# State-space output computed by channels, with rearranged first loads and last stretch, in a one-core hybrid encoder block

## The chip, the core and the metric

The kernel runs on one core of a Trainium2 chip. The metric is device time in microseconds of one execution, the median over runs. TensorE (PE in the rows) has its own weight loads (PEld); VectorE is DVE, ScalarE is ACT, GpSimd is POOL, and SyncE (SP) issues most transfers (SPq is its queue).

## The reference, cut to what matters

One encoder block over 512 tokens of width 1024, batch 1, all float32. Two token mixers work side by side on the normalised input: grouped attention (8 query heads, 2 key/value heads, 64 wide) and a two-directional state-space mixer (16 heads of 64, 2 groups, state 128, chunks of 128 tokens). Gates merge them, and a SwiGLU feed-forward part follows.

```python
y_diag = jnp.einsum("bcgls,bcgrls,bcsgrp->bclgrp", cb, decay_in, xd)
...
y_off = jnp.einsum("bclgn,bcgrpn,bcgrl->bclgrp", cc, prev, jnp.exp(a_cs))
return (y_diag + y_off).reshape(b, l, g, r, p)
...
y = y_fwd + y_bwd + d_skip.astype(f32).reshape(shp)[..., None] * xs
return rms_norm(y * jax.nn.silu(z), ssd_norm)
...
mixed = (g_attn * attn_out + g_ssd * ssd_out) @ w_out[i]
x = x + rms_norm(mixed, norm1_post[i])
gate, up = jnp.split(rms_norm(x, norm2_pre[i]) @ w_gate_up[i], 2, axis=-1)
x = x + rms_norm((jax.nn.silu(gate) * up) @ w_down[i], norm2_post[i])
```

## The kernel before

Dense products of float32 are made as three fp32r products (low by high, high by low, high by high: `mm3`, L178 to L180), so each operand is split in a high part (a cast, L144 for weights) and a low part (a subtraction, L149, on DVE or POOL; or a negation on ACT, L146, and an accumulating DMA that POOL issues, L147). Weights come in on SP's queue (L101). A unit of such work is 128 rows by 512 columns.

The stages stand in this order: query projection with norm statistics (`xT` loads, L249 to L283), keys and values, the convolution branch, the z projection woven into attention, the state-space stage (`ssd`) with gate projections as filler, `ssd_transposed` and `attn_proj`, `mix`, `out_proj`, the feed-forward part (fewer products by sums of blocks, L972), and `w_down` (seven products of blocks, L1125), which ends with the norm and the residual. A scheduler sets the order up to `mix`; from `out_proj` on PE's order is written by hand and the other engines' is the scheduler's. Within one engine instructions run in that order, so a wait stops whatever stands behind it.

**z projection** (`zproj`): tokens on partitions, tiles `z[t][n]`. **Attention**: after two heads' probabilities are transposed (L653), eight products of probabilities and values (L677) write one bank, two heads in the two halves of its 128 partitions.

**State-space stage**: there are 16 units (4 chunks, 2 groups, 2 halves of four heads). A unit makes a decay matrix E: a sum R on DVE (L757, every other unit), two products on 32 rows (L763), a selection (L766), an exponential on ACT (L767) and the product with `cb` (L768). Then four products (L815) have E as weights and 64 columns of `xs` moving, into token-major bank `sc`. Every second unit `ssd_combine` adds the states' part: per direction a product (L779), a multiplication t1 (L781, DVE), an addition to y (L782, POOL), then y plus the bank (L783) and z times y (L785). 

**`ssd_transposed`**: 32 transposes (L832) turn the result to channel-major, the split follows (L835, L836), and `attn_proj` runs between.

**The last stretch of `w_down`**: the sixth product's weights come by `raw` when they are needed. For each half token block the results are added in (`add`, L1245), squared (L155), scaled by the gain (L1257 and L1264, mostly on POOL), and `finish` makes the root (L190 to L209) and the residual (L1270) and stores.

Of the kernel before, what the change touches and what calls it, by code (L numbers as in the profile page):

```python
# [8 lines left out]
F32 = mybir.dt.float32  # L9
# [10 lines left out]
P = 128  # L20
# [40 lines left out]
class Block:  # L61
# [41 lines left out]
    def weights(self):  # L103
# [6 lines left out]
        for n in range(2):  # L110
            for i in range(4):
                yield a["w_z"][n, i], 1024, "gv"[n]
# [44 lines left out]
    def row_rstd(self, ss, dst, sqrt=False):  # L157

        V = self.V
        s2 = ss.rearrange("p (t i) -> p t i", i=2)  # L160
        v = self.tiny(NT, "rv")
        V.tensor_tensor(v, s2[:, :, 0], s2[:, :, 1], ALU.add)
        V.tensor_scalar(v, v, 1.0 / D, EPS, ALU.mult, ALU.add)
# [13 lines left out]
    def mm3(self, o, lh, ll, rh, rl, first, last):  # L177
        self.T.matmul(o, ll, rh, start=first, stop=False)  # L178
        self.T.matmul(o, lh, rl, start=False, stop=False)  # L179
        self.last_mm = self.T.matmul(o, lh, rh, start=False, stop=last)  # L180
# [53 lines left out]
    def setup(self):  # L234
# [12 lines left out]
        for k in range(KD):  # L247
            xT.append(self.slot("t", [S], name="xT"))
            self.load(xT[k], a["xT"][k * P : k * P + P])  # L249
# [13 lines left out]
        with self.tc.manual_schedule(engines=engines):  # L263
# [6 lines left out]
            for k in range(KD):  # L270
                xh.append(self.slot("q", [S], F32R, "xh"))
                xl.append(self.slot("x", [S], F32R, "xl"))
                A.mul(xh[k], xT[k], gcol[:, k : k + 1])
                A.copy(half(wh, k), half(raws, k))
                V.scalar_tensor_tensor(xl[k], xT[k], gcol[:, k : k + 1], xh[k].bitcast(F32), ALU.mult, ALU.subtract)
                last = (V if k < 1 else G).tensor_tensor(half(wl, k), half(raws, k), half(wh, k).bitcast(F32), ALU.subtract)
# [5 lines left out]
            for k in range(KD):  # L282
                for t in range(NT):  # L283
                    tok = slice(t * P, t * P + P)
                    self.mm3(pq[t], xh[k][:, tok], xl[k][:, tok], half(wh, k), half(wl, k), k == 0, k == KD - 1)
# [322 lines left out]
    def zproj(self):  # L608
        self.z = [[None, None] for _ in range(NT)]
        for n in range(2):  # L610
            w = [self.wnext(3 - i) for i in range(4)]
            for t in range(NT):
                p = self.ps("mm")
                for k in range(KD):
                    hh, hl = self.hk(self.hT, k, slice(t * P, t * P + P))
                    wh, wl = w[k // 2]
                    c = slice((k % 2) * 512, (k % 2) * 512 + 512)
                    self.mm3(p, hh, hl, wh[:, c], wl[:, c], k == 0, k == KD - 1)
                    if k == 3:
                        yield 2.6  # L620
# [835 lines left out]
```

## Time and profile before

| what | value |
| --- | --- |
| median of 3 runs | 820.66 us (820.65 to 821.98) |
| the profiled execution | 821.49 us, span 819.7 us |
| PE busy | 801.7 us, 98% of the span |
| DVE, ACT, POOL busy | 584.1, 458.9, 209.6 us |
| granted TensorE clock | 0.995 over the span, 1.00 in each stretch up to 810 us |
| chain that ended last | PE 84%, DVE 6%, ACT 3%, DMA 3%, issue 2%, POOL 2% |
| state-space stage with gates | 232 to 345 us |
| transposes and `attn_proj` | 345 to 378 us |
| last PE instruction ends | 808.8 us |

PE is busy nearly throughout, so the time is PE's work plus the start, the waits and the tail. A PE row's length is longer than the distance to the next start, since matmuls overlap; the distances between starts are what an instruction costs. An x2 in a row of PE counts records: one float32 product makes two.

### The profile page before, as it was taken

The page shows a single profiled execution, that of the slowest core. Times are in us where ns is not written, and L with a number is a line of the kernel's source. Part 1 is how long each engine was busy: PE and PEld are TensorE (multiplying, and loading weights), DVE is VectorE, ACT ScalarE, POOL GpSimd, SP SyncE. Part 2 cuts the span into 40 slices and gives each one's busy share as a digit, 9 for nine tenths or more (in the row PEclk, how much of TensorE's full clock was granted, in tenths as well). Part 3 has the DMA queues.
Part 4 walks back from the last instruction along what each step waited for, and adds up shares of the span by engine and source line. Part 5 has one row for each costly group of instructions (what it writes and reads, how often), then busy time and mean ns, then how long its engine had stood idle before and what let it go on. Part 6 is the DMA issues. An engine that isn't in the chain of part 4 may idle for free.

```text
span 819.7 us, 12211 instructions
## 1 busy us (share of the span) xinstructions
PE 801.7 (98%) x4522; PEld 674.1 (82%) x4522; DVE 584.1 (71%) x1000; ACT 458.9 (56%) x834; POOL 209.6 (26%) x161
## 2 busy tenths in 40 slices
PE   8999999999999999999999999999999999999994
PEld 7788888676667777677888899999999999888883
DVE  2979776856524556691973888888888887928987
ACT  7677875645744433285333655555555555546762
POOL 2444340000032354458450021000000000132611
PEclk9999999999999999999999999999999999999997
DMA  8657820300675653257254453666667675899542
GB/s 306 209 155 173 186 79 26 103 1 30 168 191 149 157 142 78 76 154 246 95 175 161 153 163 101 183 181 181 180 180 185 177 183 162 314 271 238 95 87 102
DMA packets 48651, 126.93 MB, mean 155 GB/s; under 512 B 5457, under 2 KB 5841, under 8 KB 48593
## 3 DMA queue, kind: packets, MB, share of 16 engines
q1 hardware_dynamic: 38048, 95.46, 33.8%
q0 software_dynamic: 10544, 30.71, 21.7%
q8 instruction: 35, 0.57, 0.3%
q14 instruction: 24, 0.19, 0.1%
HBM read 117.76 MB, written 8.39 MB: 154 GB/s over the span
## 4 chain that ended last, share of the span: by engine, by line
PE 84%; DVE 6%; ACT 3%; DMA 3%; issue 2%; POOL 2%; SPq 0%; DVEq 0%; ACTq 0%; POOLq 0%
PE sa L972 10%; PE mm L178 8%; PE mm L179 8%; PE mm L180 8%; PE sc L972 7%; PE sa L1125 4%; PE sb L1125 4%; PE mm L972 3%; PE sb L972 3%; PE mm L1125 3%; PE sc L178 3%; PE sc L179 3%; PE sc L180 3%; PE sc L677 2%; PE sb L653 2%
## 5 line engine op out<-in xcount | busy, mean ns | idle before, releaser
L144 ACT CAST whi<-raw 128x1024 fp32r<-128x1024 f32 (+3 forms) x69 | 68.1, 992 | 20.3 <-PE sc L180 9.5
L149 POOL TENSOR_TENSOR wlo<-raw,whi 128x1024 fp32r<-128x1024 f32 (+1 forms) x28 | 58.2, 2082 | 65.4 <-ACT whi L144 63.6
L178 PE MATMUL mm<-hT,wlo 128*128 128x512 f32 x176 | 73.3, 416 | 0.0
L1023 POOL DMA_DIRECT2D raw<-in_w_gu x19 | 16.3, 859 | 211.8 <-DMA raw<-in_w_gu 89.6
L180 PE MATMUL mm<-hT,whi 128*128 128x512 f32 x176 | 69.4, 394 | 0.0
L179 PE MATMUL mm<-hT,whi 128*128 128x512 f32 x176 | 68.8, 391 | 0.0
L1029 DVE TENSOR_TENSOR wlo<-raw,whi 128x512 fp32r<-128x512 f32 (+1 forms) x57 | 49.1, 889 | 17.0 <-ACT whi L1028 16.7
L1028 ACT CAST whi<-raw 128x512 fp32r<-128x512 f32 (+1 forms) x57 | 41.7, 762 | 34.5 <-PE mm L972 14.7
L972 PE MATMUL sa<-R,whi 128*128 128x256 f32 x304 | 56.4, 283 | 0.0
L147 POOL DMA_DIRECT2D wlo<-in_w_g x14 | 12.1, 862 | 145.1 <-PE mm L179 81.1
L972 PEld LDWEIGHTS sa<-R,whi 128*128 128x128 f32 x304 | 47.4, 192 | 0.0
L972 PE MATMUL sa<-R,wlo 128*128 128x256 f32 x152 | 43.0, 283 | 0.0
L178 PEld LDWEIGHTS mm<-hT,wlo 128*128 128x128 f32 x176 | 33.1, 188 | 9.4 <-issue 3.2
L179 PEld LDWEIGHTS mm<-hT,whi 128*128 128x128 f32 x176 | 33.1, 188 | 8.7 <-issue 2.4
L180 PEld LDWEIGHTS mm<-hT,whi 128*128 128x128 f32 x176 | 33.0, 188 | 7.5 <-issue 0.5
L146 ACT ACTIVATE wlo<-raw 128x1024 fp32r<-128x1024 f32 (+1 forms) x24 | 25.1, 1047 | 24.4 <-PE mm L178 24.3
L149 DVE TENSOR_TENSOR wlo<-raw,whi 128x1024 fp32r<-128x1024 f32 (+1 forms) x17 | 20.2, 1201 | 16.6 <-ACT whi L144 10.1
L972 PE MATMUL sa<-h2T,b 128*128 128x256 f32 x228 | 30.5, 283 | 0.0
L1196 DVE TENSOR_TENSOR wlo<-ch,whi 128x1024 fp32r<-128x1024 f32 x16 | 20.4, 1281 | 13.2 <-ACT whi L1195 13.1
L972 PEld LDWEIGHTS sa<-R,wlo 128*128 128x128 f32 x152 | 29.2, 192 | 0.0
L638 DVE TENSOR_REDUCE nmax<-sa 128x1 f32<-128x512 f32 x32 | 21.6, 687 | 10.2 <-PE sa L636 9.8
L155 ACT ACTIVATE junk<-z 128x512 bf16<-128x512 f32 x8 | 5.0, 628 | 42.6 <-DVE z L785 42.5
(475 smaller groups left out, 2571.4 us busy)
## 6 DMA issues: line engine op xcount, KB each, us to landing
raw<-in_w_gu SPq DMA_DIRECT2D x44, 512.0 KB, 4.4
raw<-in_w_gu POOLq DMA_DIRECT2D x19, 512.0 KB, 5.3
raw<-in_w_g SPq DMA_DIRECT2D x16, 512.0 KB, 5.9
wlo<-in_w_g POOLq DMA_DIRECT2D x14, 512.0 KB, 6.7
raw<-in_w_dn SPq DMA_DIRECT2D x14, 512.0 KB, 7.6
raw<-in_w_xbc SPq DMA_DIRECT2D x12, 512.0 KB, 5.2
ch<-in_w_dn POOLq DMA_DIRECT2D x12, 512.0 KB, 7.8
b<-in_w_gu SPq DMA_DIRECT2D x19, 256.0 KB, 5.4
```

Source lines behind the costliest of these rows:

```text
L144: self.A.copy(h[:, :n], raw[:, :n])
L146: self.A.mul(l[:, :n], raw[:, :n], -1.0)
L149: e.tensor_tensor(l[:, :n], raw[:, :n], h[:, :n].bitcast(F32), ALU.subtract)
L178: self.T.matmul(o, ll, rh, start=first, stop=False)
L179: self.T.matmul(o, lh, rl, start=False, stop=False)
L180: self.last_mm = self.T.matmul(o, lh, rh, start=False, stop=last)
L638: V.tensor_reduce(nmax, ps, AX.X, ALU.max, negate=True)
L972: self.T.matmul(dst, x, y[:, k], start=start and k == 0 and i == 0, stop=k == 3 and i == 2, skip_group_check=True)
L1028: A.copy(dst[0], src)
L1029: lo.tensor_tensor(dst[1], src, dst[0].bitcast(F32), ALU.subtract)
L1125: self.T.matmul(o, x, y, start=start and i == 0, stop=i == 2, skip_group_check=True)
L1196: V.tensor_tensor(l, src, h.bitcast(F32), ALU.subtract)
```

## The change

1. **First loads**: the first half of `w_q` is loaded ahead of the first `xT`, `norm1_pre` goes through POOL's queue, the first block is split weights first, and its first matmul is high by high.
2. **z projection** by channels: eight tiles `z[j]` of 128 channels by 512 tokens.
3. **Attention**: the eight products of one bank are issued only after the last transposition.
4. **State-space stage**: E moves (128 columns) past stationary `xs` (64 channels), two heads in the two column halves of PE, so the bank is channel-major. The states' part y stays token-major and is added into the bank by four float32 products with the identity per pair of units; the second t1 addition is on DVE. The multiplication with z is in four pieces. No transposes; the split (`ssd_out`) stands behind `attn_proj`, the squares are summed by tile on DVE, and four small products with ones add over channels.
5. **`out_proj` and the feed-forward start**: the transposes of finished token blocks (L915, `blocks`) stand half a block later, those of the last block between two plain groups, and the third group's preparation is issued earlier.
6. **`w_down`**: the sixth product's weights are loaded during the fourth; for three of the four pairs the low part is a negation on ACT and an accumulating DMA of POOL.
7. **Tail**: gains on DVE into fresh tiles, the root of blocks 0 and 1 in one pass, a first square root early, and a set order of the residuals.

```diff
+            for dst, src in loads if k else loads[::-1]:
+                self.load(dst, src)
             if k == 0:
-                self.load(gcol, a["norm1_pre"])
-            self.load(half(raws, k), a["w_q"][k // 2, :, k % 2 * 512 : k % 2 * 512 + 512])
+                G.dma_start(gcol, a["norm1_pre"])
...
+                    self.mm3(pq[t], xh[k][:, tok], xl[k][:, tok], half(wh, k), half(wl, k), k == 0, k == KD - 1, (k, t) == (0, 0))
...
+        self.z = []
+        for j in range(KD):
+            wh, wl = self.wnext()
+            p = self.ps("mm")
+            self.chan_major(p, wh, wl, self.hT, ks=range(4), last=False)
+            yield 2.6
+            self.chan_major(p, wh, wl, self.hT, ks=range(4, KD), first=False)
+            z = self.slot("z", [S], name="z")
+            self.A.copy(z, p)
+            self.z.append(z)
+            yield 2.6
...
+                for k, i in ((k, i) for k in range(NT) for i in range(2)):
+                    g = (h - 1 + i) // (NQ // NKV)
+                    with self.tc.issue_after(self.last_tr.ins):
                         self.T.matmul(po[i * HD : i * HD + HD, :], self.vt[:, k, g * HD : g * HD + HD], pts[h - 1 + i][k],
                                       start=k == 0, stop=k == NT - 1)
...
+        with self.tc.issue_after(self.last_E.ins) if self.last_E else nullcontext():
+            for p, d in ((pf, 0), (pb, 1)):
+                rr = slice(d * 64 + g * 32, d * 64 + g * 32 + 32)
+                T.matmul(p, self.lT[rr, c], r[rr], start=True, stop=True)
         E = self.slot("t", [4, P], name="E")
         pf4 = pf.rearrange("p (h l) -> p h l", h=4)
         V.copy_predicated(pf4, sel, pb.rearrange("p (h l) -> p h l", h=4))
-        A.activation(E, pf4, AF.Exp)
+        self.last_E = A.activation(E, pf4, AF.Exp)
         V.tensor_tensor(E, E, cb[:, 0].unsqueeze(1).to_broadcast([P, 4, P]), ALU.mult)
...
-            G.tensor_tensor(y, y, t1, ALU.add)
-        V.tensor_tensor(y, y, yd, ALU.add)
-        z = self.z[c][g]
-        V.tensor_tensor(z, z, y, ALU.mult)
+            (G if d == 0 and H[1] is not None else V).tensor_tensor(y, y, t1, ALU.add)
+        for i in range(4):
+            p = yd[:, i * P : i * P + P]
+            T.matmul(p, y[:, i * P : i * P + P], self.ident, start=False, stop=True, skip_group_check=True)
+        for i in range(4):
+            z = self.z[4 * g + i][:, c * P : c * P + P]
+            V.tensor_tensor(z, z, yd[:, i * P : i * P + P], ALU.mult)
...
                 h = 4 * b + j
-                T.matmul(yd[:, h * HD : h * HD + HD], E[i][:, j], self.xs[c][g][:, h * HD : h * HD + HD], start=True, stop=True)
-            yield 1.6
+                with self.tc.issue_after(begun.ins) if h > 1 else nullcontext():
+                    m = T.matmul(yd[h % 2 * HD : h % 2 * HD + HD, h // 2 * P : h // 2 * P + P], self.xs[c][g][:, h * HD : h * HD + HD],
+                                 E[i][:, j], start=h < 2, stop=False, skip_group_check=True)
+                if h == 1:
+                    begun = m
+            yield 0.8
             if b == 1:
                 self.ssd_combine(c, g, yd, pre[c, g][1], (hf[g], hb[c][g]))
-                yield 1.7
+                yield 2.2
                 if c < NT - 1:
                     hf[g] = self.step(hf[g], c, 0, g)
                     yield 0.9
...
-    def ssd_transposed(self):
         for k in range(KD):
-            p = self.ps(("sa", "sb")[k // 2 % 2])
-            for c in range(NT):
-                self.T.transpose(p[:, c * P : c * P + P], self.z[c][k // 4][:, (k % 4) * P : (k % 4) * P + P], self.ident)
+            z = self.z[k]
             hi, lo = self.hk(self.yT, k)
             g = self.gssd[:, k : k + 1]
-            self.A.mul(hi, p, g)
-            self.V.scalar_tensor_tensor(lo, p, g, hi.bitcast(F32), ALU.mult, ALU.subtract)
+            A.mul(hi, z, g)
+            V.scalar_tensor_tensor(lo, z, g, hi.bitcast(F32), ALU.mult, ALU.subtract)
+        for k in range(KD):
+            sq = self.slot("q", [S], name="sq")
+            A.activation(sq, self.z[k], AF.Square)
+            if k % 4 == 0:
+                self.ysq.append(sq)
+            else:
+                V.tensor_tensor(self.ysq[-1], self.ysq[-1], sq, ALU.add)
...
+        p = self.ps("sb")
+        a, b = self.ysq
+        self.V.tensor_tensor(a, a, b, ALU.add)
+        for t in range(NT):
+            self.T.matmul(p[:, 2 * t : 2 * t + 2], a[:, t * P : t * P + P], self.ones[:, 0:2], start=True, stop=True)
+        zss = p[:, 0 : 2 * NT].rearrange("p (t two) -> p t two", two=2)[:, :, 0]
+        return self.row_rstd(zss, self.rstd)
...
-        rest = None
+        rest = []
         for t in range(NT):
             for n in range(2):
                 for k in range(nk - ntail, nk):
                     one(k, t, n)
-            if rest:
-                rest()
-            rest = epilogue(t, po[t])
-        return rest
+                if n == 0 and t > 1:
+                    rest.pop(0)()
+            rest.append(epilogue(t, po[t]))
+        rest.pop(0)()
+        return rest.pop(0)
...
+                if u == 1 - j:
+                    (blocks2, blocks3)[j]()
             first.append((w, ps))
-            (blocks2, blocks3)[j]()
         last_hi = self.last_hi
         diag = self.row_rstd(self.xss, self.rstd, sqrt=True)
-        with self.tc.issue_after(self.last_lo.ins):
+        last_lo = self.last_lo
+        with self.tc.issue_after(last_hi.ins):
+            third = prepare_plain(2, True)
+        with self.tc.issue_after(last_lo.ins):
...
+        def sixth_weights():
+
+            for g in range(NG2):
+                t, l = new("p3", [2, 512], NG2), None
+                self.load(t, blk(g, 1, 1))
+                if g < 3:
+                    l = self.wp.tile([P, 1024], F32R, tag="raw", name=self.nm("rlo"))
+                    A.mul(l, t.rearrange("p k c -> p (k c)"), -1.0)
+                    G.dma_start(l.rearrange("p (k c) -> p k c", k=2), blk(g, 1, 1), accum_op=ALU.add)
+                b22.append((t, l))
...
-            G.tensor_tensor(c[t, n], c[t, n], gain[n], ALU.mult)
+            if t == 0:
+                A.activation(self.tiny(1, "rt"), ss[:, 0:1], AF.Sqrt)
+            V.tensor_tensor(c[t, n], c[t, n], gain[n], ALU.mult)
...
+                for i, t in enumerate(ts):
+                    gained = self.slot("t", [512], name="cg")
+                    self.last_gain = V.tensor_tensor(gained, c[t, n], gain[n], ALU.mult)
+                    c[t, n] = gained
+                for i, t in enumerate(ts):
+                    ss = half[t][1]
+                    V.tensor_scalar(v[0][:, i : i + 1], ss[:, 1:2], 1.0 / D, ss[:, 0:1], ALU.mult, ALU.add)
+                r.append(self.rsqrt(v[0], nt, True))
+                V.tensor_tensor(r[0], r[0], self.rstd[:, ts[0] : ts[0] + nt], ALU.mult)
+
+            def residual(i, t, after=()):
+                x = half[t][0]
+                for j, h in enumerate((1 - n, n)):
+                    with self.tc.issue_after(after[j].ins) if after else nullcontext():
+                        V.scalar_tensor_tensor(c[t, h], c[t, h], r[0][:, i : i + 1], x[h], ALU.mult, ALU.add)
+                    self.load(self.out[t * P : t * P + P, h * 512 : h * 512 + 512], c[t, h])
+
+            return [squares] + [lambda *after, i=i, t=t: residual(i, t, after) for i, t in enumerate(ts)]
...
         def last(t):
-            add(t, 0, y[t - 2])
-            finish(t, 0)
-
-        between = {6: lambda: finish(0, 1), 7: lambda: finish(1, 1)}
+            added = add(t, 0, y[t - 2])
+            norm, res = finish((t,), 0)
+            norm()
+            rest.append((added, self.last_gain, res))
+
+        rest = []
+
+        norm01, *res01 = finish((0, 1), 1)
+        between = {4: norm01}
...
-        product(a, lambda g: raw(g, 1, 1), a12, False, then=sums3)
+        product(a, lambda g: b22[g], a12, False, then=sums3)
...
+        for f in res01:
+            f()
+        rest[0][2](*rest[1][:2])
+        rest[1][2]()
```

How the order changes at three places. First PE in attention, at the first bank `sc` of probabilities and values (`pt` transposed probabilities, `vt` values, `hT` the input). Before:

```order
L180 MATMUL mm_1604<-whi_1114,hT_341 128x512
L677 MATMUL sc_1617<-pt_1467,vt_447 64x512
L178 MATMUL mm_1604<-whi_1171,hT_344 128x512
...
L653 MATMUL sb_1597<-cst_100,pr_1443 128x128
L677 MATMUL sc_1617<-pt_1581,vt_447 64x512
L677 MATMUL sc_1617<-pt_1474,vt_447 64x512
L677 MATMUL sc_1617<-pt_1588,vt_447 64x512
L677 MATMUL sc_1617<-pt_1481,vt_447 64x512
L677 MATMUL sc_1617<-pt_1595,vt_447 64x512
L677 MATMUL sc_1617<-pt_1488,vt_447 64x512
L677 MATMUL sc_1617<-pt_1602,vt_447 64x512
L179 MATMUL mm_1604<-wlo_1236,hT_342 128x512
```

After:

```order
L659 MATMUL sb_1603<-cst_100,pr_1443 128x128
L684 MATMUL sc_1629<-pt_1473,vt_447 64x512
L684 MATMUL sc_1629<-pt_1587,vt_447 64x512
L684 MATMUL sc_1629<-pt_1480,vt_447 64x512
L684 MATMUL sc_1629<-pt_1594,vt_447 64x512
L684 MATMUL sc_1629<-pt_1487,vt_447 64x512
L684 MATMUL sc_1629<-pt_1601,vt_447 64x512
L684 MATMUL sc_1629<-pt_1494,vt_447 64x512
L684 MATMUL sc_1629<-pt_1608,vt_447 64x512
L641 MATMUL sa_1678<-kT_432,qT_1224 128x512
```

The lone first product before the transposes has joined its seven fellows, and a z product no longer stands between.

Next PE in the state-space stage, one chunk's second unit (u are B and C, H a state, y the token-major part, mm a gate projection's bank). Before:

```order
L180 MATMUL mm_2973<-hT_342,whi_2833 128x512
L740 MATMUL sb_3002<-u_1226,u_1105 128x128
L763 MATMUL sa_3011<-R_2876,lT_1574 128x512
L763 MATMUL sa_3012<-R_2876,lT_1574 128x512
L815 MATMUL sc_2961<-xs_566,E_2957 128x64 x4
L779 MATMUL sb_3025<-H_2815,u_1162 128x512
L779 MATMUL sb_3030<-H_2312,u_1162 128x512
L178 MATMUL mm_3044<-hT_341,wlo_2907 128x512
```

After:

```order
L747 MATMUL sb_2945<-u_1226,u_1105 128x128
L788 MATMUL sb_2968<-H_2792,u_1162 128x512
...
L183 MATMUL mm_2993<-hT_343,whi_2833 128x512
L771 MATMUL sa_2955<-R_2817,lT_1580 128x512
L788 MATMUL sb_2973<-H_2311,u_1162 128x512
L828 MATMUL sc_2940<-E_2936,xs_566 64x128 x4
...
L183 MATMUL mm_2993<-hT_341,whi_2833 128x512
L794 MATMUL sc_2940<-cst_100,y_2966 128x128 x4
L183 MATMUL mm_2993<-hT_342,wlo_2834 128x512
```

E has gone from weights to moving operand with 128 columns, and the identity products follow behind filler matmuls, in the same queue as these.

Last DVE in the tail (token block 2 is `c` 7399 before and 7417 after, block 3 is 7398 and 7416). Before:

```order
L1270 SCALAR_TENSOR_TENSOR c_7401<-c_7401,ry_8255,x_1636_7965 128x512
L1270 SCALAR_TENSOR_TENSOR c_7403<-c_7403,ry_8255,x_1637_7966 128x512
L1270 SCALAR_TENSOR_TENSOR c_7400<-c_7400,ry_8276,x_1640_7974 128x512
L1270 SCALAR_TENSOR_TENSOR c_7402<-c_7402,ry_8276,x_1641_7975 128x512
L1245 TENSOR_TENSOR c_7399<-c_7399,sc_7293 128x512
L1264 TENSOR_TENSOR c_7399<-c_7399,gn_7406 128x512
...
L1245 TENSOR_TENSOR c_7398<-c_7398,sc_7319 128x512
L209 SCALAR_TENSOR_TENSOR ry_8295<-rt_8296,ry_8295 128x1
```

After:

```order
L1292 TENSOR_TENSOR c_7417<-c_7417,sc_7311 128x512
...
L1326 TENSOR_TENSOR ry_8278<-ry_8278,rstd_142 128x2
L193 TENSOR_SCALAR rn_8303<-rv_8297 128x1
...
L1332 SCALAR_TENSOR_TENSOR c_7419<-c_7419,ry_8278,x_1635_8000 128x512
...
L1332 SCALAR_TENSOR_TENSOR cg_8271<-cg_8271,ry_8278,x_1636_8001 128x512
...
L1332 SCALAR_TENSOR_TENSOR c_7418<-c_7418,ry_8278,x_1640_8011 128x512
...
L1332 SCALAR_TENSOR_TENSOR cg_8273<-cg_8273,ry_8278,x_1641_8012 128x512
L1326 TENSOR_TENSOR ry_8304<-ry_8304,rstd_142 128x1
L1292 TENSOR_TENSOR c_7416<-c_7416,sc_7337 128x512
```

Block 2's addition now stands ahead of the four residuals of blocks 0 and 1 instead of behind them, and block 3's follows them directly.

## Rows read from the trace of the kernel before

**Rows 1.** Page part 1: engine, busy us (share of the span), instructions.

```profile
PE 801.7 (98%) x4522; PEld 674.1 (82%) x4522; DVE 584.1 (71%) x1000; ACT 458.9 (56%) x834; POOL 209.6 (26%) x161
```

**Rows 2.** Stretches: span us, then each engine's busy us, granted PE clock, DMA.

```profile
232.00:345.00 113.00, 112.75 (x504) 82.52 (x502) 61.55 (x91) 42.70 (x74) 46.56 (x38) 1.00 0.50 127
790.00:800.00 10.00, 10.00 (x45) 8.13 (x44) 9.46 (x15) 7.35 (x16) 2.63 (x2) 1.00 0.00 1
```

**Rows 3.** Waits of PE by line and releaser: total us, times, longest us.

```profile
PE sb L178 <- DVE hT L184: 0.9, 1, 0.9
...
PE mm L178 <- ACT at L693: 0.8, 2, 0.6
...
PE sb L915 <- DVE m L957: 0.7, 1, 0.7
...
PE sa L179 <- DVE h2T L184: 0.3, 1, 0.3
...
PE sc L1125 <- DVE wlo L1196: 0.6, 1, 0.6
...
PE mm L179 <- POOL wlo L149: 0.3, 1, 0.3
```

**Rows 4.** Timeline of the start: start us, length us, engine, line, tiles [idle before <-releaser].

```profile
3.69 0.72 ACT L273 ACTIVATE xh<-xT,gcol 128x512 fp32r<-128x512 f32 x1 [1.45 <-DMA gcol<-in_norm_pre]
...
6.19 0.50 PE L178 MATMUL sc<-whi,xl 128*128 128x512 f32 x1 [0.92 <-ACT whi L274]
```

**Rows 5.** Timeline, PE, around two attention outputs.

```profile
148.34 1.07 PE L677 MATMUL sc<-pt,vt 128*64 128x512 f32 x2
...
149.35 0.50 PE L178 MATMUL mm<-whi,hT 128*128 128x512 f32 x1
...
173.45 3.65 PE L677 MATMUL sc<-pt,vt 128*64 128x512 f32 x16
...
177.04 0.50 PE L178 MATMUL mm<-whi,hT 128*128 128x512 f32 x1
```

**Rows 6.** Timeline, PE, two places of the state-space stage.

```profile
243.68 0.49 PE L763 MATMUL sa<-R,lT 32*128 32x512 f32 x1
...
244.10 0.50 PE L180 MATMUL mm<-hT,whi 128*128 128x512 f32 x1
...
298.72 0.38 PE L740 MATMUL sb<-u,u 128*128 128x128 f32 x2
...
299.03 0.50 PE L763 MATMUL sa<-R,lT 32*128 32x512 f32 x2
...
299.46 1.10 PE L815 MATMUL sc<-xs,E 128*128 128x64 f32 x8
...
300.40 1.94 PE L779 MATMUL sb<-H,u 128*128 128x512 f32 x4
```

**Rows 7.** Timeline, POOL and DVE, one unit of that stage.

```profile
302.36 1.60 POOL L782 TENSOR_TENSOR y<-y,t 128x512 f32<-128x512 f32 x1 [1.69 <-DVE t L781]
...
304.44 1.53 DVE L757 TENSOR_TENSOR R<-rT,cst 128x512 fp32r<-128x512 f32 x1
...
307.14 0.69 DVE L783 TENSOR_TENSOR y<-y,sc 128x512 f32<-128x512 f32 x1 [1.18 <-POOL y L782]
```

**Rows 8.** Timeline, PE, the transposes of the states' output.

```profile
358.03 0.60 PE L832 MATMUL sb<-cst,z 128*128 128x128 f32 x4
...
358.71 0.49 PE L832 MATMUL sb<-cst,z 128*128 128x128 f32 x3
```

**Rows 9.** Timeline, the tail: DVE and PE.

```profile
807.61 0.69 DVE L1245 TENSOR_TENSOR c<-c,sc 128x512 f32<-128x512 f32 x1
...
808.41 0.39 PE L1125 MATMUL sc<-whi,as 128*128 128x512 f32 x1
...
810.71 0.68 DVE L1245 TENSOR_TENSOR c<-c,sc 128x512 f32<-128x512 f32 x1
...
814.99 1.41 DVE L1270 SCALAR_TENSOR_TENSOR c<-c,ry,x 128x512 f32<-128x512 f32 x2
```

More of the change, by code (lines that the diff above doesn't have):

```diff
@@ L1 @@
 import numpy as np
-from contextlib import ExitStack
+from contextlib import ExitStack, nullcontext
 from itertools import chain
@@ L109, in weights @@
             yield a["w_xbc"][j], 1024, "g" if j < 3 else "d"
-        for n in range(2):
-            for i in range(4):
-                yield a["w_z"][n, i], 1024, "gv"[n]
+        for j in range(KD):
+            yield a["w_z"][j], 1024, "gv"[j // 4]
         for j in range(2 * KD):
@@ L159, in row_rstd @@
         V = self.V
[L160 removed]
         v = self.tiny(NT, "rv")
[L162 to L163 removed]
+        if ss.shape[-1] == 2 * NT:
+            s2 = ss.rearrange("p (t i) -> p t i", i=2)
+            V.tensor_tensor(v, s2[:, :, 0], s2[:, :, 1], ALU.add)
+            ss = v
+        V.tensor_scalar(v, ss, 1.0 / D, EPS, ALU.mult, ALU.add)
         V.tensor_copy(dst, self.rsqrt(v, NT, sqrt))
@@ L175, in spread, with mm3 @@
         return row
[L177 to L180, printed above, removed]
+    def mm3(self, o, lh, ll, rh, rl, first, last, hi_first=False):
+        three = [(ll, rh), (lh, rl), (lh, rh)]
+        if hi_first:
+            three.reverse()
+        for i, (x, y) in enumerate(three):
+            self.last_mm = self.T.matmul(o, x, y, start=first and i == 0, stop=last and i == 2)
     def hilo(self, hi, lo, src):
@@ L248, in setup @@
             xT.append(self.slot("t", [S], name="xT"))
-            self.load(xT[k], a["xT"][k * P : k * P + P])
+            loads = [(xT[k], a["xT"][k * P : k * P + P]),
+                     (half(raws, k), a["w_q"][k // 2, :, k % 2 * 512 : k % 2 * 512 + 512])]
+            for dst, src in loads if k else loads[::-1]:
+                self.load(dst, src)
             if k == 0:
-                self.load(gcol, a["norm1_pre"])
-            self.load(half(raws, k), a["w_q"][k // 2, :, k % 2 * 512 : k % 2 * 512 + 512])
+                G.dma_start(gcol, a["norm1_pre"])
             if k == 4:
@@ L272, in setup @@
                 xl.append(self.slot("x", [S], F32R, "xl"))
[L273 to L276, printed above, removed]
+                xhi = lambda: A.mul(xh[k], xT[k], gcol[:, k : k + 1])
+                whi = lambda: A.copy(half(wh, k), half(raws, k))
+                xlo = lambda: V.scalar_tensor_tensor(xl[k], xT[k], gcol[:, k : k + 1], xh[k].bitcast(F32), ALU.mult, ALU.subtract)
+                wlo = lambda e: e.tensor_tensor(half(wl, k), half(raws, k), half(wh, k).bitcast(F32), ALU.subtract)
+                if k == 0:
+                    whi(), xhi(), wlo(V), xlo()
+                else:
+                    xhi(), whi(), xlo()
+                    last = wlo(G)
                 for t, i in xs[XAT[k] : XAT[k + 1]]:
@@ L608, in zproj @@
     def zproj(self):
[L609 to L620, printed above, removed]
-                z = self.slot("z", [512], name="z")
-                self.A.copy(z, p)
-                self.z[t][n] = z
-                yield 2.6
+        self.z = []
+        for j in range(KD):
+            wh, wl = self.wnext()
[7 more added lines that the diff above has]
+            yield 2.6
     def softmax_rows(self, h):
@@ L1088, in ffn @@
             else:
-                with self.tc.issue_after(last_hi.ins):
-                    w = prepare_plain(j, True)
+                w = third
                 ps = [self.ps("sa") for _ in range(2)]
@@ L1359, in run @@
             for z in self.z:
-                for i in range(2):
-                    self.A.activation(z[i], z[i], AF.Silu)
+                self.A.activation(z, z, AF.Silu)
         self.weave(self.ssd(), 41.0, self.gates(range(NG, 2 * KD)), 5.2 * (2 * KD - NG))
-        self.ssd_transposed()
         self.attn_proj()
+        self.ssd_out()
         self.mix()
@@ L1425, in lay_out @@
         "w_xbc": rows(xbc, P, KD)[:, 0],
-        "w_z": rows(z, 512, 2),
+        "w_z": rows(z, P, KD)[:, 0],
         "w_g": rows(gt, P, KD)[:, 0],
```

58 lines of the change are left out of this document (25 added, 33 removed).

## Prediction

> **What bounds the kernel now.** I first read the busy times of the engines: PE works 801.7 of 819.7 us [rows 1], the next engine, DVE, 584.1. The time is therefore PE's own work plus what PE cannot fill: the start, some waits and the tail. Second, the table by stretch: in the state-space stage PE is busy 112.75 of 113 us [rows 2], so there is no idle time to win there, only work to save, and every new wait costs in full. Third, the list of PE's waits by releaser [rows 3]: the longest are short, 0.3 to 0.9 us, one at each seam. Fourth, the timelines of the places that the change touches, read by distances from one start to the next. A dense fp32r product costs 0.222 us (45 in 10.00 us, [rows 2]).
>
> The sum is made against the profiled execution, 821.49 us. It lies 0.83 above the median of the three runs, 820.66; the difference that I find is taken off the median.
>
> **Start.** ACT's first high part waits 1.45 us for `norm1_pre`, and the first real product starts at 6.19 after waiting 0.92 for the weights' high part [rows 4]. The change puts the weights in front and takes the small load off SP. At most the 0.92 goes. But at 40 us PE still waits 0.9 for DVE's low parts [rows 3], and these come from loads that all have the same total length; what is gained earlier may only make that wait longer. I take -0.5, bounds 0 and -0.9.
>
> **z projection.** The same 192 products in another order; one wait of 0.3 on a low part made by POOL [rows 3] stands in its first group. I take -0.3, bounds 0 and -0.3. The squares and the split that this layout brings run on ACT and DVE behind `attn_proj`, whose 96 products cover 96 x 0.222 = 21.3 us; some 16 operations of 0.7 each on ACT and on DVE are 11 us per engine, so they hide. Without that cover the first product of `mix` would wait for one split, about 1.5 us.
>
> **Attention.** Eight products of probabilities and values, issued together, take 177.04 - 173.45 = 3.59 us, that is 0.90 for two heads side by side. A lone first product, split off ahead of the transposes, takes 149.35 - 148.34 = 1.01 [rows 5], and the seven that are left still need four passes. By the order three of four groups were split before and none is now: 3 x 1.0 = -3.0. The lower bound of the gain is 3 x (1.01 - 0.45) = 1.7, if a lone product only loses its partner.
>
> **State-space stage, the decay products.** Before, a unit of four products with E as weights takes 300.40 - 299.46 = 0.94 [rows 6], 16 units 15.0 us. After, two heads lie side by side with 128 columns moving. If they behave as attention's, a pair of a quarter of the columns costs 0.90/4 = 0.22, a unit 0.45. Against that stands the surplus of the lone product, 1.01 against 0.90 for a full pair: 0.11 or so for getting in, and a like amount for getting out. I take 0.65 a unit: 16 x 0.29 = -4.6. Bounds: 0.45 (-7.8), and 1.01, where even a short unit costs what the lone long product does (+1.1).
>
> Here a rule of the Trainium skill speaks against the change. The trace has entered and left the half-width arrangement in attention at 1.01 for a lone product and 0.90 a pair [rows 5]. TensorEngine Tiling (Array Packing), Tiling Modes, Key Properties, says that changing the tiling mode drains TensorE. The trace agrees only so far as a small surplus shows. By the rows' middle the units save 4.6, by the rule at its hardest they lose 1.1; that is the second rival below.
>
> **Identity products.** There are 32 of 128x128 by 128 columns in float32. Nearest rows: four products of the old unit with the same size of weights, 0.235 each, and the lone one of the same shape, 299.03 - 298.72 = 0.31 [rows 6]. I take 0.235, since they come four at a time: +7.5, bounds 7.5 and 9.9. Four tiny products for the sums of squares cost no more than 0.235 each: +0.9.
>
> **Transposes.** Four transposes and one fp32r product lie between two starts 358.71 - 358.03 = 0.68 apart [rows 8]; less 0.222 that is 0.115 a transpose, and 32 of them go: -3.7. With them go the two waits of 0.8 in all on evictions in that stretch [rows 3]: -0.8.
>
> **Split decay pairs.** The two 32-row products of a decay matrix take 299.46 - 299.03 = 0.43 together and 244.10 - 243.68 = 0.42 for one alone [rows 6]. By the order 2 of 16 pairs stood apart before and 5 do now: 3 x 0.41 = +1.2. Adjacent again they would cost nothing more.
>
> **New waits there.** The identity products stand in PE's queue ahead of filler and need y: t1 on DVE (a form like the 0.69 of [rows 7]), an addition on POOL (1.60), a second t1 and an addition on DVE (0.69 each). That is 3.0 us from the last state product where it has to go through POOL, with 1.53 more where an R stands in DVE's queue [rows 7]. By the order, 6 to 13 filler products lie between, 1.3 to 2.9 us, plus other small work. Most of the 8 groups fit barely, one or two do not. A wait there holds all filler behind it, and the gates' evictions with it. I take +2.0, bounds 0 and 8. The longer DVE work (four short multiplications for one) hides under 113 - 61.55 us of free DVE [rows 2].
>
> The stage together: -4.6 + 7.5 + 0.9 - 3.7 - 0.8 + 1.2 + 2.0 = +2.5.
>
> **Feed-forward start.** PE waits 0.7 for a block that is to be transposed and 0.3 for low parts of `h2T` [rows 3]. Half a block of products ahead of each covers both: -1.0, bounds 0 and -1.4. On DVE the third group's preparation moves ahead; what it delays is not needed before the groups that are already prepared have run.
>
> **Sixth product of `w_down`.** PE waits 0.6 for a low part there [rows 3], late since the weights are loaded late. Early loads remove it: -0.6, bounds 0 and -1.2. Three ACT negations and three accumulating DMAs on POOL's queue are added; that queue loses the gains, which go to DVE, four of 0.69 each, in a stretch where three splits leave DVE.
>
> **Tail.** PE ends at 808.41 + 0.39 = 808.8. Block 2's addition starts at 807.61 and block 3's at 810.71, 1.9 late, since residuals of earlier blocks stand ahead on DVE [rows 9]. By the order 24 products follow block 2's last one, 24 x 0.222 = 5.3 us, and now DVE does in them the addition (0.69), the gain, four residuals (2 x 1.41) and a chain of short ones of about 1.0: 5.2 us, so block 3's addition starts about 0.3 after PE's end, -1.6. From there to the last residual it was 814.99 - 810.71 = 4.28; one residual instead of two ahead of the gain gives -0.4. Together -2.0, bounds 0 and -2.6.
>
> **Sum:** -0.5 - 0.3 - 3.0 + 2.5 - 1.0 - 0.6 - 2.0 = -4.9. The profiled execution would be 816.6, the median 820.66 - 4.9 = 815.8.
>
> **Rivals.** First, the better end: units at 0.45 and no waits in the stage, 3.2 + 2.0 less, 810.6. For it: attention shows nearly full pairing [rows 5]. Against it: the chains above. Second, entry and exit eat the pairing, a unit costs 1.01: 5.7 more, 821.5, no change. For it: short products; against it: the surplus of a lone one is only 0.11. Third, the seams do not shrink, since another releaser is as late at the start, the feed-forward start and the sixth product: 2.1 more, 817.9. Fourth, slower: the identity products wait for y in all 8 groups. Without any wait the sum is -6.9, so slower by 0.2% needs 8.5 us of waits, 1.1 a group. With R ahead everywhere and the least filler, 3.0 + 1.53 - 1.3 = 3.2 would be missing, 26 us; with half of that, 1.6, it is 12.8, 10.8 more than I took: 826.6. For it: PE runs in order, and the stage has no idle time now. Against it: y's chain starts ahead of a whole unit in most groups. That the attention groups stay split is excluded by the order.
>
> **Chances.** Forecast 0.53, better end 0.12, no pairing gain 0.10, seams stay 0.15, slower 0.10. The range 810.3 to 820.5 runs from the better end to just short of the case without pairing. A measurement of this kernel can tell about 0.2%, 1.6 us, from no change: faster by that is below 819.0, and the first, second and fourth of these cases lie there, 0.80 in all. Same takes 0.10, slower 0.10.
>
> **What would show it.** Right: attention's products in four groups of eight; units of L828 at 0.6 to 0.7 from start to next start; identity groups of four at 0.9 to 1.0; an addition of block 3 within 0.5 of PE's end. Wrong: PE idle ahead of L794 with DVE or POOL as releaser, several us in all; units at 0.9 or more; a new wait of PE at the start of `mix`; the last residual more than 6 us after PE's end.

## The result and the profile after

The changed kernel takes 833.64 us (833.14 to 837.17), the kernel before 820.65; the ratio is 1.0164, 95% interval 1.0134 to 1.0194. Forecast was 815.8, range 810.3 to 820.5: wrong in sign and outside the range. Busy time and waits of PE after, as [rows 1] and [rows 3] of before (page part 1; list of PE's waits):

```profile
PE 805.5 (97%) x4562; PEld 671.9 (81%) x4562; DVE 586.8 (71%) x1029; ACT 460.5 (55%) x829; POOL 187.2 (23%) x151
```

```profile
PE sb L173 <- DVE diag L167: 7.4, 1, 7.4
PE sc L794 <- DVE y L791: 5.2, 4, 2.8
PE sa L183 <- DVE g L1126: 2.6, 1, 2.6
```

The waits of [rows 3] at L915, at L1125 and for `at` (L693) are gone, and three waits that did not exist before take 15.2 us in all. Where the 12.1 us between the spans (819.7 and 831.8) arise, from the starts of the same PE instruction in both traces:

| stretch | change | forecast |
| --- | --- | --- |
| start to the first decay product (start, z, attention) | -5.2 | -3.8 |
| state-space stage and `attn_proj` | +9.8 | +2.5 |
| `mix` | +10.6 | 0 |
| `out_proj`, then feed-forward part | -0.9, +1.7 | -1.0 |
| `w_down` | -1.4 | -0.6 |
| last PE instruction to the end | -2.5 | -2.0 |

**The wait in `mix`.** The scale of the state-space norm goes through a chain of fifteen short operations on DVE to `diag`, which PE spreads over the partitions (L173) behind the first unit of `mix`. In the kernel before, `diag` was ready 11 us before PE needed it:

```profile
371.62 0.69 DVE L166 TENSOR_TENSOR diag<-cst,rstd 128x512 f32<-128x512 f32 x1
...
383.50 1.02 PE L172 MATMUL sb<-diag,ones 128*128 128x512 f32 x2
```

Timeline after (columns as in [rows 4]):

```profile
382.74 0.16 DVE L164 TENSOR_SCALAR rv<-sb 128x4 f32<-128x4 f32 x1 [11.34 <-PE sb L864]
...
383.88 2.44 POOL L148 TENSOR_TENSOR wlo<-raw,whi 128x1024 fp32r<-128x1024 f32 x1
383.89 2.46 DVE L204 TENSOR_SCALAR ry<-rv 128x4 int32<-128x4 int32 x1
...
387.49 2.40 POOL L148 TENSOR_TENSOR wlo<-raw,whi 128x1024 fp32r<-128x1024 f32 x1
387.63 2.27 DVE L210 TENSOR_TENSOR rt<-ry 128x4 f32<-128x4 f32 x1
...
390.33 0.16 DVE L210 TENSOR_TENSOR rt<-ry 128x4 f32<-128x4 f32 x1
...
392.65 2.33 POOL L148 TENSOR_TENSOR wlo<-raw,whi 128x1024 fp32r<-128x1024 f32 x1
...
392.75 2.79 DVE L167 TENSOR_TENSOR diag<-cst,rstd 128x512 f32<-128x512 f32 x1
395.68 2.05 PE L173 MATMUL sb<-diag,ones 128*128 128x512 f32 x2 [7.38 <-DVE diag L167]
```

DVE had been idle for 11.34 us: the squares were long done, and only the four small products (L864), which stand behind all of `attn_proj` in PE's queue, were missing. From there the chain takes 12.8 us, against one unit of `mix`, 24 x 0.222 = 5.3 us, as cover. The same line L210 lasts 2.27 us while POOL runs and 0.16 when it does not, and the long one ends at 389.90, POOL's at 389.89. I call such an operation held. The stall has a second price, by the table of stretches after:

```profile
385.00:390.00 5.00, 3.31 (x15) 2.42 (x13) 4.90 (x4) 1.68 (x3) 4.89 (x3) 1.00 0.68 251
390.00:395.00 5.00, 0.00 (x0) 0.00 (x0) 4.69 (x10) 1.56 (x2) 3.56 (x2) 0.66 0.75 254
395.00:400.00 5.00, 4.32 (x8) 2.85 (x9) 2.15 (x4) 2.23 (x5) 0.52 (x1) 0.50 0.85 313
400.00:405.00 5.00, 5.00 (x19) 3.98 (x18) 4.88 (x6) 1.58 (x3) 2.52 (x2) 0.82 0.04 15
```

The granted clock (third value from the end) falls to 0.50, the lower of TensorE's two levels, and products there start 0.43 apart instead of 0.23:

```profile
400.08 0.63 PE L183 MATMUL sc<-yT,wlo 128*128 128x512 f32 x1
...
400.51 1.06 PE L183 MATMUL sc<-yT,whi 128*128 128x512 f32 x2
```

**The waits for y.** One of the four groups of identity products that wait, after (compare [rows 7]):

```profile
295.19 1.38 POOL L791 TENSOR_TENSOR y<-y,t 128x512 f32<-128x512 f32 x1
...
295.80 2.32 DVE L764 TENSOR_TENSOR R<-rT,cst 128x512 fp32r<-128x512 f32 x1
296.42 1.14 POOL L783 TENSOR_TENSOR y<-xs,dcol 128x512 f32<-128x512 f32 x1
298.05 0.68 DVE L791 TENSOR_TENSOR y<-y,t 128x512 f32<-128x512 f32 x1
...
298.78 1.16 PE L794 MATMUL sc<-cst,y 128*128 128x128 f32 x8 [1.19 <-DVE y L791]
```

R has two operands from SBUF, and here it is held by two POOL operations in a row. In the other three groups y's own last addition is held by POOL's start of another y, as here (in the last group R is held as well, 1.44):

```profile
277.67 1.43 POOL L783 TENSOR_TENSOR y<-xs,dcol 128x512 f32<-128x512 f32 x1 [0.70 <-DVE dcol L754]
278.12 1.53 DVE L791 TENSOR_TENSOR y<-y,t 128x512 f32<-128x512 f32 x1
```

**The feed-forward start**, ACT and DVE after:

```profile
504.50 1.05 ACT L1056 CAST whi<-raw 128x1024 fp32r<-128x1024 f32 x1 [4.45 <-DMA raw<-in_w_gu]
...
509.32 0.58 ACT L175 COPY row<-mm 128x512 f32<-128x512 f32 x1
...
511.08 0.68 DVE L1126 TENSOR_TENSOR g<-sa,row 128x512 f32<-128x512 f32 x1
```

The scale row, whose product PE had started at 502.49, is copied at 509.32, in ACT's queue behind a cast that waited 4.45 us for weights.

**What the new work costs by itself.** Sums of distances from each start to the next, from the first state product to the first of `mix`:

| products | before | after |
| --- | --- | --- |
| with E, 16 units | 14.6 | 9.4 |
| identity / transposes | 2.9 | 7.4 |
| sums over channels | 0 | 0.8 |
| decay pairs on 32 rows | 8.3 | 9.0 |
| from states to y, and the states' own | 17.9 | 18.8 |
| B with C | 3.0 | 2.5 |
| dense, with the waits ahead of what follows | 106.1 | 114.8 |

### The profile page after: what moved, and what is told of

Its sections match the earlier page's. It is cut to its first block, busy times and chain, and to the rows that moved or that the text cites. A ratio compares the mean times of both kernels' runs of the same rounds, so it can differ in the third digit from the quotient of the medians.

```text
span 831.8 us, 12309 instructions
## 1 busy us (share of the span) xinstructions
PE 805.5 (97%) x4562; PEld 671.9 (81%) x4562; DVE 586.8 (71%) x1029; ACT 460.5 (55%) x829; POOL 187.2 (23%) x151
## 4 chain that ended last, share of the span: by engine, by line
PE 85%; DVE 9%; DMA 3%; issue 2%; ACT 1%; SPq 0%; DVEq 0%
PE mm L183 25%; PE sa L1000 10%; PE sc L183 7%; PE sc L1000 7%; PE mm L1156 4%; PE sb L1156 4%; PE sa L1156 4%; PE mm L1000 3%; PE sb L1000 3%; PE sa L183 3%; PE sc L1156 2%; PE sb L659 2%; PE sc L684 2%; PE sb L183 1%; DMA x<-in_x 1%
## 5 line engine op out<-in xcount | busy, mean ns | idle before, releaser
L183 PE MATMUL mm<-hT,whi 128*128 128x512 f32 x480 | 154.7, 398 | 0.0
L183 PEld LDWEIGHTS mm<-hT,whi 128*128 128x128 f32 x480 | 90.3, 190 | 22.0 <-issue 4.7
L183 PE MATMUL mm<-hT,wlo 128*128 128x512 f32 x240 | 100.0, 417 | 0.0
L148 POOL TENSOR_TENSOR wlo<-raw,whi 128x1024 fp32r<-128x1024 f32 (+1 forms) x28 | 59.9, 2141 | 88.7 <-ACT whi L143 84.6
L183 PEld LDWEIGHTS mm<-hT,wlo 128*128 128x128 f32 x240 | 45.4, 189 | 13.0 <-issue 4.9
L146 POOL DMA_DIRECT2D wlo<-in_w_g x14 | 12.1, 867 | 147.3 <-ACT wlo L145 137.3
L183 PE MATMUL sc<-hT,whi 128*128 128x512 f32 x96 | 29.7, 390 | 0.0
L1000 PEld LDWEIGHTS sa<-h2T,b 128*128 128x128 f32 x228 | 28.7, 192 | 0.0
L774 DVE COPY_PREDICATED sa<-cst,sa 128x512 f32<-128x512 uint32 x16 | 11.1, 691 | 25.0 <-PE sa L771 25.0
L1000 PE MATMUL sc<-R,whi 128*128 128x256 f32 x152 | 28.2, 283 | 0.0
```

The costliest lines, as they stand in the source:

```text
L148: e.tensor_tensor(l[:, :n], raw[:, :n], h[:, :n].bitcast(F32), ALU.subtract)
L183: self.last_mm = self.T.matmul(o, x, y, start=first and i == 0, stop=last and i == 2)
L1000: self.T.matmul(dst, x, y[:, k], start=start and k == 0 and i == 0, stop=k == 3 and i == 2, skip_group_check=True)
```

## Experiments: the three waits

**The chain earlier.** The first experiment undoes nothing but the place of the four small products:

```diff
-        self.attn_proj()
+        self.attn_proj(range(6))
         self.ssd_out()
+        self.ydiag = self.y_rstd()
+        self.attn_proj(range(6, KD))
```

> The changed kernel with one move: the four small products that sum the squares, and the root chain behind them, stand ahead of the last two attn_proj blocks instead of behind them, 24 products (5.4 us) earlier in PE's queue. In the changed kernel PE waits 7.4 us for diag in mix and runs slowly for some us after it. Theory late start (the chain of 13 us from 382.7 to 395.5 is covered by one mix product only): the wait falls from 7.4 to about 2, the slow clock behind it goes, time 833.6 - 7 to -9 = 825 to 827. Theory port (the chain is only long since DVE's small operations are held while POOL runs): the same start, the chain still 10 to 13 us long in this run, so a rest of 1 to 3 us stays. Rival, that DVE has no room before: no change, 833.6.

Measured 826.38 (1.0071, 1.0045 to 1.0097), 7.3 less. By the starts of its trace 6.0 of them arise in `mix`. Another 2.2 arise ahead of it and are not the edit's: the waits for y are 5.2 as in the changed kernel, but this time no slow clock follows the last of them. Its wait for `diag` and its chain:

```profile
PE sb L173 <- DVE diag L167: 2.9, 1, 2.9
```

```profile
375.08 0.16 DVE L164 TENSOR_SCALAR rv<-sb 128x4 f32<-128x4 f32 x1 [5.12 <-PE sb L863]
...
388.12 0.69 DVE L167 TENSOR_TENSOR diag<-cst,rstd 128x512 f32<-128x512 f32 x1
```

It starts 7.7 us earlier and is as long, 13.7 us. So lateness is one half of the cause, and the length does not come from the place.

**POOL out of the way.** The other half: the place of the changed kernel, but no POOL arithmetic beside the chain.

```diff
-            yield a["w_sp"][j], 1024, "g"
+            yield a["w_sp"][j], 1024, "d"
...
-            G.tensor_tensor(at, at, ga, ALU.mult)
+            (V if j < 4 else G).tensor_tensor(at, at, ga, ALU.mult)
```

> The changed kernel with POOL emptied while the root chain runs: the low parts of w_sp come by an ACT negation and an accumulating DMA instead of a POOL subtraction (2.4 us each), and the first four products of at and ga are on DVE instead of POOL (1.3 us each). The chain starts where it did, at 382.7. Theory port: its twelve small operations take 0.16 each and diag 0.69, the chain is 3.5 to 5 us instead of 13, the 7.4 us wait for diag is gone, time 833.6 - 9 to -11.5 = 822 to 825. Theory late start alone: the chain is long by itself, the wait stays at 5 us or more, time 830 or more.

Measured 832.19 (1.0125, 1.0087 to 1.0162), so the forecast of the time failed, though the wait for `diag` did vanish:

```profile
383.36 0.16 DVE L204 TENSOR_SCALAR ry<-rv 128x4 int32<-128x4 int32 x1
...
385.74 0.69 DVE L167 TENSOR_TENSOR diag<-cst,rstd 128x512 f32<-128x512 f32 x1
...
386.87 0.76 PE L183 MATMUL mm<-yT,wlo 128*128 128x512 f32 x1 [3.82 <-DMA wlo<-in_w_sp]
```

The chain that starts at 383.09 is through at 386.4, 3.3 us instead of 12.8: POOL made the other 9.5. But the low parts now come by transfers that land late, and PE waits 3.8 for one of them ahead of the first unit of `mix`. Without that wait PE would have come to `diag` at about 383.1 + 5.3 = 388.4, so it would have been ready in time all the same.

**The state-space stage without POOL's arithmetic** (three `G.tensor_tensor` become `V.tensor_tensor`: y's start, y's first addition, the states' decay):

> The changed kernel with the state-space stage's additions and multiplications of POOL (first addition to y 1.3 to 1.6 us, y's start 1.0 to 1.5, state decay 1.1 to 1.5) on DVE. Theory port: DVE's operations with two operands from SBUF lose the time for which they are held (y's last addition 1.53 to 0.68, R 2.3 to 0.68), so the four waits of identity products for y, 5.2 us in all, fall under 1.5 and the slow clock at 333 to 337 goes; time 833.6 - 4 to -6.5 = 827 to 829.6. Theory length: DVE is the bottleneck of y's chain, so 22 more operations of 0.68 on DVE leave the waits at 5 us or more; time 833.6 or more.

Measured 826.75 (1.0066, 1.0045 to 1.0086), 6.9 less, part of it from a `diag` wait that was shorter in its trace (5.3; the next run has 5.4 with nothing changed near it). Line R in the changed kernel and then here (count, shortest, median and longest ns), and the waits:

```profile
L764 DVE TENSOR_TENSOR R<-rT,cst x8: 679/682/2320, 216.7 to 330.0; 128x512 fp32r<-128x512 f32 x8
```

```profile
L764 DVE TENSOR_TENSOR R<-rT,cst x8: 675/682/689, 217.5 to 328.4; 128x512 fp32r<-128x512 f32 x8
```

```profile
PE sc L794 <- DVE y L791: 0.5, 1, 0.5
```

More work on DVE made y earlier: 5.2 us of waits became 0.5. The theory that DVE is simply too full falls. Two things went at once, though: the holds, and POOL's own length in y's chain (1.27 to 1.57 us an addition, against 0.68 on DVE). No run parts them.

**The feed-forward start: two candidates.** First the third group's early preparation undone:

```diff
-            third = prepare_plain(2, True)
...
-                w = third
+                with self.tc.issue_after(last_hi.ins):
+                    w = prepare_plain(j, True)
```

> The changed kernel with one edit of the feed-forward start undone: the third plain group is prepared where the kernel before did it, behind the first two. Theory early preparation (its buffers and its place on ACT and DVE delay the eviction that the third group's bank waits for): the 2.6 us wait of sa at L1126 goes, time 833.6 - 2.0 to -2.7 = 831 to 831.6. Theory transfers (the loads of that stage land later than they did since the stage before was slowed): the wait stays between 2 and 3 us, time 833.6.

Measured 833.35 (1.0149, 1.0130 to 1.0167); the wait for g stays 2.6. The early preparation is not it. That the time is the same is chance in part: the trace has 4.7 less up to the end of `mix`, which the edit does not touch, and 4.5 more from the feed-forward part on, which was not followed up. Then the row ahead of the cast:

```diff
-            with self.tc.issue_after(last_hi.ins):
+            with self.tc.issue_after((self.row_copied if j == NPLAIN else last_hi).ins):
                 w = prepare(j)
```

> The changed kernel with one order set: the first combined group of the feed-forward part is prepared only after ACT has copied the row of the norm's scale, where the changed kernel puts that group's first cast, which waits 4.45 us for a transfer, ahead of the copy. Theory queue (the scale row stands behind a cast that waits for weights, g and so the bank of the third plain group come late): the row is copied about 3 us earlier, the 2.6 us wait of sa for g falls under 0.5, time 833.6 - 2 to -2.7 = 831 to 831.6. Theory transfers: the group's weights are late in any case and the wait only moves to the first product of that group, sc at L1000, time 833.6 within 0.7.

Measured 829.28 (1.0090, 1.0059 to 1.0121), 4.4 less; the wait for g is gone, and the cast that stood first waits 0.24:

```profile
502.20 0.58 ACT L175 COPY row<-mm 128x512 f32<-128x512 f32 x1
503.03 1.05 ACT L1056 CAST whi<-raw 128x1024 fp32r<-128x1024 f32 x1 [0.24 <-DMA raw<-in_w_gu]
503.49 0.69 DVE L1126 TENSOR_TENSOR g<-sa,row 128x512 f32<-128x512 f32 x1
```

So it was the queue and not the transfers. By the starts of its trace 2.8 of the 4.4 arise in the feed-forward part and 1.2 in `mix`, where the wait for `diag` was 6.7 this time.

## Experiments: the parts, and all waits mended

**All three orders mended**, with the sums ahead of the last four `attn_proj` blocks:

> The changed kernel with three orders mended and all of its own parts kept: the sums of squares and the root chain stand ahead of the last four attn_proj blocks (10.8 us of cover more), the state-space stage's POOL operations are on DVE, and the scale row is copied ahead of the first combined group's casts. Theory of three waits (diag 7.4 with slow clock behind it, y 5.2 with slow clock, g 2.6 are what made it slower than forecast): their cost of about 11.5, 6.5 and 2.5 goes nearly whole, time 833.6 - 17 to -20.5 = 813 to 816.5, below the kernel before. Rival, that the units and identity products themselves are dear or that work moved to DVE makes new waits: 819 or more.

Measured 816.26 (0.9935, 0.9916 to 0.9954): 17.4 less, at the edge of what was expected. No wait for `diag` is left: the chain takes 4.4 us, since it now stands ahead of most of POOL's work for `mix`. PE waits 1.3 for the squares instead. **The state-space part of the kernel before**, all else changed:

> The changed kernel with its state-space part undone: z projection by tokens, E as weights, transposes, squares summed by tokens, as in the kernel before; the first loads, attention's grouped products, the feed-forward start, the sixth product and the tail stay changed. Theory of three waits (the other parts gain what was forecast, -7.4 in all, and only the feed-forward start gives 1.6 back): 820.7 - 5.5 to -8 = 812.5 to 815. Rival, that the other parts gain less than the trace suggests: 817 or more. In either case the difference to 833.6 is what the state-space part costs with its waits, and is to be compared with the three fixes.

Measured 815.00 (0.9924, 0.9896 to 0.9953), with the wait for g still there, 3.0. So the state-space part with its waits cost 18.6 us, and even mended it was no gain yet. **The two parts alone** on the kernel before, first attention's order and then the changed `w_down`:

> The kernel before with one edit of the change alone: the eight products of probabilities and values are issued after the last transposition. By the rows, three split groups of 1.0 us each: 820.7 - 3.0 = 817.7, within 0.7. Rival, that the lone product hides under something else: 820.7.

> The kernel before with the change's w_down alone: the sixth product's early weights and the new tail. Theory additive (a shorter tail by 2.5 and a removed wait of 0.6 to 1.4, whatever stands ahead): 820.9 - 3.1 to -3.9 = 817.0 to 817.8. Rival (the gains on DVE and the POOL transfers give some back): 819 or more.

Attention's order measured 818.18 (0.9960, 0.9944 to 0.9976), 3.2 less than the 821.43 of the kernel before beside it. `w_down` measured 818.13 (0.9964, 0.9952 to 0.9977), 2.5 less than the 820.67 beside it, a little under what its profile shows (a tail of 8.8 us from the last PE start instead of 11.3, and 1.4 less in `w_down`).

**Which form of the state-space part is better?** The old one with the row first:

> The changed kernel with the state-space part of the kernel before and the scale row copied ahead of the first combined group's casts. The kernel with the old part alone came to 815.0 and still waits 3.0 us for g in the feed-forward start. Theory queue: that wait goes, time 815.0 - 2.5 = 812.5, within 0.8, clearly below both kernels. Rival, transfers: the wait only moves, 815.

Measured 812.04 (0.9891, 0.9877 to 0.9906), the fastest of all; PE's longest wait is the 1.1 at the start that before has too. The new form first with the sums ahead of three blocks:

> The changed kernel with the three orders mended, the sums of squares ahead of the last three attn_proj blocks instead of the last four. With four, 816.3, PE waits 1.3 us for the last sum of squares and the stretch around it is granted 0.94 of the clock. Theory (the waits that are left, with the slow clock behind them, keep it above the old state-space part, not the price of the new products): the 1.3 us wait goes and the clock with it, 816.3 - 1.3 to -3 = 813.3 to 815. Rival (the small products now end too late for the row in mix): a wait for diag of up to 2 us, 816.3 or more.

Measured 816.37 (0.9943, 0.9930 to 0.9955), as the rival had it. The chain, held by POOL in eight of its fifteen operations and 16.1 us long, was late again:

```profile
PE sb L173 <- DVE diag L167: 2.5, 1, 2.5
```

Then the same with POOL's work beside the chain on DVE:

```diff
-            yield a["w_sp"][j], 1024, "g"
+            yield a["w_sp"][j], 1024, "vvvvgggg"[j]
...
-            G.tensor_tensor(at, at, ga, ALU.mult)
+            (V if j < 4 else G).tensor_tensor(at, at, ga, ALU.mult)
```

> The kernel with the three orders mended and the sums ahead of the last three attn_proj blocks (816.4; PE waits 2.5 us for diag there, at a chain of over 17 us held by POOL), with the first four low parts of w_sp and the first four products of at and ga on DVE itself instead of POOL. Theory port: DVE does that work in 1.2 and 0.7 us instead of being held 2.4 and 1.3 for it, so even with it in its own queue the chain ends 4 to 8 us earlier, the wait for diag and the slow clock behind it go, time 816.4 - 3 to -4.5 = 812 to 813.4, level with the old state-space part (812.0). Rival (any other work on DVE delays the chain as much, held or not): the wait stays at 2 us or more, 816.

Measured 812.83 (0.9910, 0.9894 to 0.9927). The chain, with five larger operations in its own queue:

```profile
366.52 0.16 DVE L164 TENSOR_SCALAR rv<-sb 128x4 f32<-128x4 f32 x1 [2.41 <-PE sb L863]
...
368.43 1.23 DVE L148 TENSOR_TENSOR wlo<-raw,whi 128x1024 fp32r<-128x1024 f32 x1
...
373.04 0.69 DVE L167 TENSOR_TENSOR diag<-cst,rstd 128x512 f32<-128x512 f32 x1
```

It takes 7.2 us, and no wait for `diag` is left. With that the two forms of the state-space part are level: 812.83 against 812.04, with ratios to the kernel before whose intervals overlap.

## Why the prediction was wrong, step by step

- **z projection.** The step that failed most. I priced the split and the squares that move behind `attn_proj`, found them hidden, and named one split of 1.5 us as the price without cover. I did not follow the root chain that hangs on the squares. Its four products stand behind `attn_proj`, so its cover is not the 21.3 us of `attn_proj` but one unit of `mix`, 5.3 us, and it lasts 12.8. I had named a new wait at the start of `mix` as a sign of being wrong, but gave it no term: 0, measured +10.6 in `mix`, 7.4 of it the wait and most of the rest the slow clock. Two blocks earlier it is 6.0 less; four blocks earlier, with the stage's POOL work on DVE, `mix` takes 44.4 us, against 44.5 before. The term for the z products themselves was -0.3. From the first product of the convolution branch to the first state product the changed kernel takes 176.2 us and the one with the old z and state-space part 176.8, so about -0.6.
- **New waits there.** Term +2.0, bounds 0 and 8; the waits were 5.2, and with the slow clock behind the last of them 8.1: from the first state product to the first of `mix` it is 162.6 us, and 154.5 with POOL's arithmetic on DVE. The mechanism was the fourth rival's, in four groups and not in eight; its 826.6 held nothing for `mix`. The mis-sizing has a reason: I took 1.53 us for R from [rows 7] as its price and 0.69 for y's last addition. R lasts 0.68 when POOL is idle; the 1.53 was already a hold, by a POOL operation that [rows 7] leave out:

```profile
303.93 1.48 POOL L731 TENSOR_TENSOR H<-H,dec 128x512 f32<-128x512 f32 x1
```

An R of 2.32, and a last addition to y of 1.53 in three of the four groups, I did not reckon with.

- **The rule that I passed over.** The Trainium skill, SBUF — State Buffer, Who interferes with whom, says that only the port pair that DVE and GpSimd share causes contention, and that it is an exclusive lock. The trace agrees: short operations of DVE end with the POOL operation beside them, 0.16 against 2.27 us on one line. I weighed a rule on TensorE's tiling instead.
- **Feed-forward start.** Term -1.0, measured -0.9 in `out_proj` and +1.7 in the feed-forward part. The waits that I counted did go; that the scale row would stand behind a cast that waits for weights could be read from the order of ACT, where I looked at PE and DVE only. With the row first the feed-forward part takes 1.1 less than before, so the term of -1.0 for both was too small rather than wrong.
- **Decay products.** Term -4.6, measured 14.6 - 9.4 = -5.2, 0.59 a unit. The pairing works for 128 columns, and the second rival, 1.01 a unit, is refuted here.
- **Identity products, sums, transposes, split pairs.** +7.5, +0.9, -3.7, +1.2; measured +7.4 (6.7 where no clock fell), +0.8, -2.9, +0.7. The price of the identity products was read from products of half the columns; that it comes near is luck. Not in my list: the products from the states to y, +1.8, the states' own, -0.9, and B with C, -0.5. Most of these is a matter of booking. Ahead of a dense product the last record of a float32 product takes 0.03, and that dense product 0.63 instead of 0.23; ahead of others the record takes 0.4 to 0.5. Of the products to y six stood ahead of a dense one before and three do now; of the states' own, four and six.
- **So the bare work** of the stage was forecast at 2.5 - 2.0 = +0.5, and the mended kernels show about +1.8 (154.4 with the sums ahead of three blocks, 152.7 in the old form, from the first state product to the first of `mix`). Of these, +1.3 lie in the dense products, and why is open. The forecast failed on waits, far more than on work.
- **Attention.** -3.0, measured -3.2 alone, and four groups of eight in the trace.
- **Sixth product and tail.** -0.6 and -2.0, measured -1.4 and -2.5 in the trace, alone -2.5 together in the times. Block 3's addition starts 0.03 after PE's end.
- **Start.** -0.5; unsettled. The first product starts between 5.1 and 6.8 us in the kernels with the new start and between 6.2 and 6.6 in those with the old one.

## What to carry to other kernels

When a change moves the producer of a reduced value, follow that value to its last consumer and count the cover of the whole chain from the point where its input really stands in the queue, not from where its data are ready. A DVE duration read beside a POOL operation may be a hold: look for the shortest instance of the same line before it is used as a price. And a wait that empties PE can be paid twice, by the wait and by the slow clock behind it: the 7.4 us for `diag` came to 10.6, while the 2.6 for g left the clock at 1.00.

## What was not expected of the hardware

A DVE operation of four columns can last as long as the POOL operation beside it: 2.46 us instead of 0.16. Where POOL worked without a break, step after step was held by the next POOL operation, so a chain of fifteen operations that takes 3.3 us alone took 12.8 (six held), 13.7 (seven) and 16.1 (eight). Moving work from POOL to the fuller engine DVE made that engine's results earlier (y's waits 5.2 to 0.5 us). And after an idle PE of 7.4 us the granted clock stood at 0.50. Around the last wait for y, 2.8 us, it was 0.85 and 0.81 in the two stretches below; behind the same wait of 2.8 in the first experiment it stayed at 1.00.

```profile
330.00:335.00 5.00, 2.19 (x11) 1.95 (x11) 3.33 (x6) 0.00 (x0) 2.35 (x2) 0.85 0.01 3
335.00:340.00 5.00, 5.00 (x22) 3.17 (x21) 1.30 (x5) 1.10 (x2) 0.48 (x1) 0.81 0.04 16
```
